# Squares of x on ScalarE and VectorE, most of them in the second column group: a hybrid decoder step on one core

## The chip, the core and the metric

The kernel runs on 1 core of one Trainium2 chip. The metric is the device time of one execution in microseconds; before, it is 1715.74 us, the median of 3 runs (1714.48 to 1716.54). A measurement of this kernel can tell a change of about 0.2% (3.4 us) from none.

## The reference

One step of a decoder layer for 256 prompt rows and 8 sample rows (264 columns in the kernel, which holds everything transposed). Each row is normed, projected to 13 324 columns, mixed by three kinds of head, and projected back:

```python
def rmsnorm(x, g):
    xf = x.astype(F32)
    y = xf * lax.rsqrt(jnp.mean(xf * xf, axis=-1, keepdims=True) + EPS) * g.astype(F32)
...
    aq, ak, av, az, mq, mk, mv, mi, mf, mo, mz, cu, cv, cz = split_projection(
        jnp.einsum('btd,de->bte', hn, w_in))
...
    y = jnp.concatenate([a_out.astype(F32) * jax.nn.silu(az.astype(F32)),
                         m_out * jax.nn.silu(mz.astype(F32)),
                         c_out * jax.nn.silu(cz.astype(F32))], axis=-1).astype(hn.dtype)
    out = jnp.einsum('bte,ed->btd', y, w_out).astype(hn.dtype)
```

The mean of x*x over 4096 features is what this change is about. The factor of the norm is the same for all columns of a row, so the kernel multiplies x by the gain alone, projects it, and applies the factor (`rstd`) to the result.

## The kernel before, in words

The weights come in 34 column groups of 512 columns: 26 of the first projection (`wi`) and 8 of the second (`wo`). A group is worked off in 16 chunks (`NCH`) of two blocks of 128 input features (`KK`), so a chunk is one load of 128 x 1024 weights. `steps` lists all pairs (g, c) of group and chunk, and n counts them through.

Each product is made of three passes with numbers split in two. ScalarE rounds the weights (`wh<-wf`), VectorE takes the rest (`wl<-wf,wh`), and for each of 4 column blocks and 2 feature blocks TensorE multiplies wh by xh, wh by xl and wl by xh: 24 matmuls a chunk, which add up in four PSUM tiles (`mp`) over the 16 chunks of a group. `split_w(n + 2)` stands two chunks ahead of the matmuls; the tiles wf, wh and wl have three buffers each. `load_w(n + 4)` waits on SP's queue until VectorE has made the wl of chunk n + 1, because that frees the buffer.

The first group has more to do, since x comes in with it. Chunk by chunk SP loads two blocks of x into `yb` (`load_x`), ScalarE makes `xh<-yb,sms` (two instructions), and VectorE makes `xl<-yb,sms,xh` (two instructions). `split_x` also squares the two blocks on GpSimd (`sq2<-yb`, in the page `sq`) and adds them up on GpSimd (`acc<-acc,sq`). When the first group is through, `first_norm` sums `acc` over the partitions on TensorE and makes `rstd`. The first group's results went out of PSUM unscaled (`evac` with g == 0: `yb<-mp` on ScalarE), so `first_norm` scales and gates these four tiles; every later group multiplies by rstd as it leaves PSUM (`et<-mp,rstd` on VectorE) and a `gated` task finishes it.

Tiles of yb are used twice: results of group 0 go into tiles 12 to 15, which held the x of chunks 6 and 7, and those of group 1 into tiles 16 to 19, the x of chunks 8 and 9.

The gates of the matrix memory need 12 more columns of the projection. `gate_loads` clears `wgs` on GpSimd and loads `wgf`, `gate_prep` multiplies by the gain on VectorE, and `gate_mm` issues 32 small matmuls (`gps<-yb,wgs`) in the first group. The rest of the kernel's constants (`sms[:, 32:]`: identity, masks, gains) are one load.

Within an engine instructions run in the order written; side tasks (`spawn`) are resumed between the column blocks of the main loop by a tally of issued work. Lines in the profile are mostly L201, the helper through which every operation is issued, so tile names tell the work apart.

Of the kernel before, what the change touches and what calls it, by code (L numbers as in the profile page):

```python
# [12 lines left out]
AF = mybir.ActivationFunctionType  # L13
ALU = mybir.AluOpType
# [6 lines left out]
KT = D // P  # L21
# [6 lines left out]
EPS = 1e-6  # L28
# [38 lines left out]
KK = 2  # L67
# [3 lines left out]
NCH = KT // KK  # L71
# [17 lines left out]
def body(tc, xt, wi, wg, wo, sm, kc, vc, c0, wst, w00, bs, cgain, cbias,  # L89
# [3 lines left out]
    with ExitStack() as ctx:  # L93
# [53 lines left out]
        def tt(eng, out, a, b, op):  # L147
            eng.tensor_tensor(out, a, b, op)
# [9 lines left out]
            return n  # L158

        class Eng:  # L160
            """An engine whose issued work is tallied, so that dependent work is issued when due."""

            def __init__(self, eng, key, fixed, per):
                self.e, self.k, self.f, self.p = eng, key, fixed, per
# [44 lines left out]
        DQ = nc.sync  # L209
# [4 lines left out]
        def load_w(n):  # L214
            if n >= len(steps):
                return
            g, c = steps[n]
            src = wi[g] if g < NG else wo[g - NG]
            t = wp.tile([P, KK, 512], F32, name="wf", bufs=3)
            DQ.dma_start(t, src[:, KK * c:KK * c + KK, :])  # L220
            wf_t[n] = t
# [18 lines left out]
        def split_x(s):  # L240
            if s >= NCH:
                return
            for k in range(KK * s, KK * s + KK):
                if s == 0:
                    V.tensor_scalar(xh[:, k], yb[:, k], sc("ng", k), None, ALU.mult)
                else:
                    A.activation(xh[:, k], yb[:, k], AF.Copy, scale=sc("ng", k))
                V.scalar_tensor_tensor(xl[:, k], yb[:, k], sc("ng", k), xh[:, k].bitcast(F32),
                                       ALU.mult, ALU.subtract)
            sl = yb[:, KK * s:KK * s + KK, :]  # L250
            if s == 0:
                tt(G, acc, sl, sl, ALU.mult)
            else:
                q = ph.tile([P, KK, T], F32, name="sq2", tag="vT")
                tt(G, q, sl, sl, ALU.mult)
                tt(G, acc, acc, q, ALU.add)

        def rsqrt(out, x, scale, v, t):
            """out = (x * scale + EPS) ** -0.5, with one Newton step; v and t are scratch."""
            n = out.shape[0]  # L260
            V.tensor_scalar(v, x, -0.5 * scale, -0.5 * EPS, ALU.mult, ALU.add)
            A.activation(t, x, AF.Sqrt, scale=scale, bias=epsc[:n, 0:1])
            newton(out, v, t)
# [69 lines left out]

        st = {}

# [1 line left out]
        def gate_loads():  # L337
            wgf = ph.tile([P, KT, 12], F32, name="wgf", tag="big", bufs=2)
            wgs = ph.tile([P, KT, 32], F32, name="wgs", tag="big", bufs=2)
            G.memset(wgs, 0.0)  # L340
            DQ.dma_start(wgf, wg)
            st["wgf"], st["wgs"] = wgf, wgs
# [83 lines left out]
            rel()  # L426
            st.update(gd=gd, encol=encol, gcol=gcol)

# [1 line left out]
        def head_loads(h):  # L430
            cb = ph.tile([P, TS, DV + 1], F32, name="cb", bufs=2)
            while h >= 2 and ("done", h - 2) not in st:
# [146 lines left out]
                    tt(V, dst, dst, src[:, :, j], ALU.mult)  # L579
            rel()  # L580

# [1 line left out]
        def attn_kv(g):  # L583
            kT, vT, vtok = st["kT"], st["vT"], st["vtok"]
            ps = yield from acq()
# [136 lines left out]
                tt(V, ys, ys, pnb[:, 24 * g:24 * g + 24].rearrange("p (b j) -> p j b", j=3), ALU.mult)  # L722
            rel()

# [1 line left out]
        def gmlp_prep():  # L726
            wm = ph.tile([P, CG, P], F32, name="wm")
            Z = ph.tile([P, CG, P], F32, name="Z")
# [76 lines left out]
                yield  # L805
                DQ.dma_start(dst, TM[:n, b])

# [1 line left out]
        def gated(kind, i, t):  # L809
            yield 1.5 if kind != "cv" else None  # L810
            s = t
# [29 lines left out]
        def first_norm():  # L841
            yield
            ps = yield from acq()
            yield from wait("es", 2)
            norm_factor(ps, [acc[:, 0], acc[:, 1]])
            rel()
            give("es")
            give("es")
            yield
            for i in range(4):  # L850
                y = yb[:, S_A + i]
                yield from wait("es")
                s = hp.tile([P, T], F32, name="es", bufs=2)
                tt(V, y, y, rstd, ALU.mult)
                yield
                A.activation(s, y, AF.Sigmoid)
                yield
                tt(V, y, y, s, ALU.mult)
                give("es")

        def evac(g, kind, i, ps):
            if g == 0:
                A.activation(yb[:, S_A + i], ps, AF.Copy)
            elif kind in ("mo", "mz", "az", "cz", "cu", "cv"):
                while not free["et"]:
                    tick(True)
                free["et"] -= 1
                t = hp.tile([P, T], F32, name="et", bufs=4)
                tt(V, t, ps, rstd, ALU.mult)
                spawn(gated(kind, i, t), urgent)  # L870
            elif kind == "mq":
                q = ph.tile([P, T], F32, name="q")
                tt(V, q, ps, rstd, ALU.mult)
                st["mq", i] = q
            elif kind == "mk":
                k = ph.tile([P, T], F32, name="k")
                V.scalar_tensor_tensor(k, ps, ISQ, rstd, ALU.mult, ALU.mult)
                st["mk", i] = k
            elif kind == "mv":
                h, f = i  # L880
                if f == 0:
                    st["mv", h] = ph.tile([P, 2, T], F32, name="vt")
                tt(V, st["mv", h][:, f], ps, rstd, ALU.mult)
            elif kind in ("ak", "av"):
                if "kT" not in st:
                    st["kT"] = ph.tile([P, AKV, T], F32, name="kT")
                    st["vT"] = ph.tile([P, AKV, T], F32, name="vT")
                    st["vtok"] = ph.tile([P, AKV, 2, P], F32, name="vtok")
                    st["qs"] = ph.tile([P, AH, TS], F32, name="qs")
                tt(V, st["kT" if kind == "ak" else "vT"][:, i], ps, rstd, ALU.mult)  # L890
            elif kind == "aq":
                q = ph.tile([P, T], F32, name=f"aq{i % 4}")
                V.scalar_tensor_tensor(q, ps, ISQ, rstd, ALU.mult, ALU.mult)
                V.tensor_copy(st["qs"][:, i], q[:, TP:])
                st["aq", i] = q
# [54 lines left out]

        last = []

# [1 line left out]
        def drain():  # L954
            while gens or urgent:
                tick(True)
# [12 lines left out]
        load_w(1)  # L969
        load_x(2)  # L970
        load_w(2)
        DQ.dma_start(sms[:, 32:], sm[:, 32:])
        gate_loads()
        warm = px.tile([P, 512], F32, name="mx")
        for i in range(NWARM):
            PE.matmul(warm[:, :P], ones, ones, start=True, stop=True)
# [7 lines left out]
        for n, (g, c) in enumerate(steps):  # L984
            if c == 0:
                before_group(g)
                main_ps = [pm.tile([P, 512], F32, name="mp") for _ in range(4)]
            if g == 0:
                load_x(c + 4)
            load_w(n + 4)  # L990
            if g == 0:
                split_x(c + 2)
            split_w(n + 2)
            if g == NG:
                for i in (KK * c, KK * c + 1):
                    if i < S_C:
                        nc.sync.dma_start(yb[:, i, :], xt[:, i, :])
            if g == NG - 1 and c >= 1 and KK * (c - 1) < S_C:
                for i in range(KK * (c - 1), KK * c):
                    split_y(i)  # L1000
            if g == NG and KK * c + KK > S_C:
                while ("c", KK * c + KK - 1 - S_C) not in st:
                    tick(True)
            wh, wl = wh_t.pop(n), wl_t.pop(n)
            for j in range(4):
                tick()
                out = main_ps[j][:, :T]
                for kk in range(KK):
                    k = KK * c + kk
                    s = slice(P * j, P * j + P)  # L1010
                    PE.matmul(out, wh[:, kk, s], xh[:, k], start=(k == 0), stop=False)
                    PE.matmul(out, wh[:, kk, s], xl[:, k], start=False, stop=False)
                    PE.matmul(out, wl[:, kk, s], xh[:, k], start=False, stop=(k == KT - 1))
                if c == NCH - 1:
                    if g < NG:
                        kind, i, _ = GROUPS[g][j]
                        evac(g, kind, i, out)
                    else:
                        evac_out(4 * (g - NG) + j, out)
            if g == 0 and c == 4:  # L1020
                gate_prep()
            if g == 0 and c >= 7:
                for m in ([(c - 7) // 2] if c < NCH - 1 else range((c - 7) // 2, KT // 4)):
                    if c % 2:
                        gate_mm(m)
            if c == NCH - 1 and g < NG:
                if g == 0:
                    spawn(chain(first_norm(), gate_sum()), urgent)
                after_group(g)
        drain()  # L1030
# [133 lines left out]
```

## Time and profile before

| | |
|---|---|
| runs, median (lowest to highest) | 1715.74 us (1714.48 to 1716.54) |
| profiled execution, span from first to last instruction | 1715.0 us (the profile gives no other time of that execution) |
| TensorE busy | 1682.7 us, 98% |
| VectorE / ScalarE / GpSimd busy | 928.2 / 733.2 / 125.2 us |
| HBM traffic | 191 GB/s over the span |
| first matmul of group 0, of group 1 | 4.96 us, 73.92 us |

TensorE's busy time takes in matmuls at half clock, so a share of 98% does not say that it ran at its peak. The median of the three runs lies 0.7 us above the span, which is inside the spread of the runs.

### The profile page before, as it was taken

How to read it: one execution, taken by the hardware profiler on the slowest of the kernel's cores; microseconds unless marked ns; L12 is line 12 of the kernel's file. 1: busy time of each engine (PE TensorE's matmuls, PEld its weight loads, DVE VectorE, ACT ScalarE, POOL GpSimd, SP SyncE). 2: the span in 40 equal slices, each digit the busy share in tenths (PEclk: the TensorE clock that was granted, in tenths of full speed). 3: DMA queues.
4: the chain of work that ended last, by engine and by line, in shares of the span. 5: the costliest groups of instructions: out<-in, count | busy, mean ns of one | idle time of the engine just before them, and what ended most of it. 6: DMA issues, size and time to landing. Idle time of an engine off the chain costs nothing.

```text
span 1715.0 us, 32547 instructions
## 1 busy us (share of the span) xinstructions
PE 1682.7 (98%) x13754; PEld 1664.7 (97%) x13754; DVE 928.2 (54%) x1262; ACT 733.2 (43%) x954; POOL 125.2 (7%) x113
## 2 busy tenths in 40 slices
PE   7999999999999999999999999999999999999995
PEld 7899999999999999999999999999999999999995
DVE  8755444555554455555655566444566554444445
ACT  4444433444444334344444444334454443444442
POOL 7300000000000000000101000000100030000002
PEclk9999999999999999999999999999999999999998
DMA  6566668555556666667677767666666666565663
GB/s 225 176 181 175 183 184 264 180 165 155 161 160 176 182 182 176 208 191 237 214 232 220 240 213 221 177 181 184 201 177 216 198 196 190 180 184 177 181 183 145
DMA packets 102178, 328.92 MB, mean 192 GB/s; under 512 B 11090, under 2 KB 24328, under 8 KB 102032
## 3 DMA queue, kind: packets, MB, share of 16 engines
q1 hardware_dynamic: 101072, 326.04, 62.7%
q8 instruction: 107, 1.75, 0.4%
q10 hardware_dynamic: 960, 0.81, 0.1%
q14 instruction: 39, 0.32, 0.1%
HBM read 314.20 MB, written 12.60 MB: 191 GB/s over the span
## 4 chain that ended last, share of the span: by engine, by line
PE 94%; DVE 3%; DMA 1%; issue 1%; ACT 0%; SPq 0%; DVEq 0%; ACTq 0%
PE mp L201 90%; PE mx L201 3%; DVE wl L201 1%; DVE xl L201 1%; DVE yb L201 1%; DMA wf<-wi 1%; DMA wf<-wo 1%; PE sn L201 0%; ACT wh L201 0%; PE gps L201 0%; DVE rstd L201 0%; DVE TM L201 0%; DVE mvs L201 0%; ACT L201 0%; DVE es L201 0%
## 5 line engine op out<-in xcount | busy, mean ns | idle before, releaser
L201 PE MATMUL mp<-xh,wl 128*128 128x264 f32 x4352 | 1240.6, 285 | 12.6 <-DVE wl L201 12.6
L201 PE MATMUL mp<-xh,wh 128*128 128x264 f32 x4352 | 1251.5, 288 | 0.6 <-ACT wh L201 0.6
L201 PE MATMUL mp<-xl,wh 128*128 128x264 f32 x4352 | 1238.2, 285 | 0.0
L201 DVE TENSOR_TENSOR wl<-wf,wh 128x1024 fp32r<-128x1024 f32 (+1 forms) x545 | 695.0, 1278 | 750.8 <-ACT wh L201 746.0
L201 ACT ACTIVATE wh<-wf 128x1024 fp32r<-128x1024 f32 (+1 forms) x545 | 575.0, 1058 | 839.1 <-PE mp L201 734.2
L201 PEld LDWEIGHTS mp<-xh,wl 128*128 128x128 f32 x4352 | 820.6, 189 | 15.2 <-DVE wl L201 15.0
L201 PEld LDWEIGHTS mp<-xh,wh 128*128 128x128 f32 x4352 | 820.7, 189 | 7.2 <-issue 5.0
L201 PEld LDWEIGHTS mp<-xl,wh 128*128 128x128 f32 x4352 | 820.8, 189 | 0.4
L201 POOL TENSOR_TENSOR acc<-acc,es 128x264 f32<-128x264 f32 x29 | 21.9, 754 | 417.1 <-ACT es L201 415.1
L201 POOL TENSOR_SCALAR_AFFINE_SELECT tmp<-bc 128x128 f32<-128x128 f32 x12 | 4.7, 412 | 496.6 <-DMA bc<-gd 496.6
L201 DVE SCALAR_TENSOR_TENSOR xl<-yb,sms,xh 128x264 fp32r<-128x264 f32 x32 | 35.1, 1135 | 1.2 <-ACT xh L201 1.1
L201 ACT ACT_TABLE_LOAD x25 | 32.1, 1283 | 3.4 <-DVE ar L201 2.2
L201 POOL MEMSET pad<- 128x1024 f32 x2 | 1.9, 950 | 406.4 <-PE mx L201 406.4
L201 POOL TENSOR_TENSOR acc<-acc,sq 128x528 f32<-128x528 f32 x15 | 24.0, 1603 | 1.2
L201 ACT ACTIVATE es<-et 128x264 f32<-128x264 f32 x36 | 14.0, 420 | 21.4 <-DVE yb L201 18.1
L201 POOL TENSOR_TENSOR cb<-cb,bc 128x2056 f32<-128x2056 f32 x6 | 21.7, 3616 | 0.0
L201 POOL TENSOR_TENSOR sq<-yb 128x528 f32<-128x528 f32 x15 | 20.6, 1375 | 9.8 <-DMA yb<-xt 9.1
L201 ACT ACTIVATE es<-yb 128x264 f32<-128x264 f32 x33 | 13.6, 412 | 16.3 <-DVE yb L201 16.3
L201 DVE TENSOR_TENSOR et<-mp,rstd 128x264 f32<-128x264 f32 x56 | 20.3, 423 | 0.0
L201 DVE SCALAR_TENSOR_TENSOR cb<-vb,wsk,cb 128x257 f32<-128x257 f32 x48 | 20.1, 480 | 0.0
L201 ACT ACTIVATE bias<-bias,ar 128x128 f32<-128x128 f32 (+1 forms) x24 | 10.7, 448 | 21.4 <-DVE ar L201 21.2
L201 ACT ACTIVATE xh<-yb 128x264 fp32r<-128x264 f32 x32 | 12.1, 412 | 17.7 <-DVE yb L201 17.7
(178 smaller groups left out, 471.6 us busy)
## 6 DMA issues: line engine op xcount, KB each, us to landing
wf<-wi SPq DMA_DIRECT2D x415, 512.0 KB, 3.6
wf<-wo SPq DMA_DIRECT2D x128, 512.0 KB, 3.6
cb<-c SPq DMA_DIRECT2D x12, 514.0 KB
o_cs<-cb SPq DMA_DIRECT2D x12, 514.0 KB, 6.4
vb<-vsd SPq DMA_DIRECT2D x12, 512.0 KB, 5.2
yb<-xt SPq DMA_DIRECT2D x34, 132.0 KB, 3.7
yb<-xt SPq DMA_DIRECT2D x15, 264.0 KB, 5.3
o_y<-yb SPq DMA_DIRECT2D x7, 528.0 KB, 3.1
```

Source lines behind the costliest of these rows:

```text
L201: return fn(*a, **k)
```

## The change

Four things change. The squares are made on ScalarE and added on VectorE by a function of its own, `square_x`; it is called for two pieces at the end of group 0 and for fourteen in the chunks of group 1, the pieces whose tiles are overwritten first. `first_norm` is started after group 1, so the first two groups leave PSUM unscaled (`yb<-mp`) and it finishes eight tiles, not four. The loads of `wgf` and of `sms[:, 32:]` move from the start to chunks 6 and 12 of group 0. And `gate_prep` and `gate_mm` stand later in group 0.

```diff
@@ split_x, and a new function
-            sl = yb[:, KK * s:KK * s + KK, :]
-            if s == 0:
-                tt(G, acc, sl, sl, ALU.mult)
+
+        SQ = [6, 7, 8, 9] + [s for s in range(NCH) if s not in (6, 7, 8, 9)]
+
+        def square_x(n):
+
+            if n >= NCH:
+                return
+            sl = yb[:, KK * SQ[n]:KK * SQ[n] + KK, :]
+            if n == 0:
+                A.activation(acc, sl, AF.Square)
             else:
                 q = ph.tile([P, KK, T], F32, name="sq2", tag="vT")
-                tt(G, q, sl, sl, ALU.mult)
-                tt(G, acc, acc, q, ALU.add)
+                A.activation(q, sl, AF.Square)
+                tt(V, acc, acc, q, ALU.add)
...
@@ first_norm
-            for i in range(4):
+            for i in range(8):
...
@@ evac
-            if g == 0:
+            if g <= 1:
                 A.activation(yb[:, S_A + i], ps, AF.Copy)
...
@@ main sequence
         load_w(2)
-        DQ.dma_start(sms[:, 32:], sm[:, 32:])
-        gate_loads()
...
             load_w(n + 4)
+            if (g, c) == (0, 6):
+                gate_loads()
+            if (g, c) == (0, 12):
+                DQ.dma_start(sms[:, 32:], sm[:, 32:])
             if g == 0:
                 split_x(c + 2)
...
-            if g == 0 and c == 4:
+            if n == NCH - 6:
                 gate_prep()
-            if g == 0 and c >= 7:
-                for m in ([(c - 7) // 2] if c < NCH - 1 else range((c - 7) // 2, KT // 4)):
-                    if c % 2:
-                        gate_mm(m)
+            if g == 0 and c >= NCH - 4:
+                for m in range(2 * (c - NCH + 4), 2 * (c - NCH + 4) + 2):
+                    gate_mm(m)
+            if NCH - 3 <= n <= NCH - 2:
+                square_x(n - NCH + 3)
+            elif n >= NCH:
+                square_x(n - NCH + 2)
             if c == NCH - 1 and g < NG:
-                if g == 0:
+                if g == 1:
                     spawn(chain(first_norm(), gate_sum()), urgent)
```

On GpSimd the program begins as follows (lines with - are those of before, lines without a sign stand in both; acc and sq are the sums and the squares).

```order
 L201 MEMSET epsc 128x1 x2
 L201 MEMSET ones 128x128
 L201 MEMSET wgs 128x1024
-L201 ISA
-L201 TENSOR_TENSOR acc<-yb 128x528
-L201 TENSOR_TENSOR sq_138<-yb 128x528
-L201 TENSOR_TENSOR acc<-acc,sq_138 128x528
-L201 TENSOR_TENSOR sq_156<-yb 128x528
-L201 TENSOR_TENSOR acc<-acc,sq_156 128x528
```

The pairs go on to the sixteenth piece; all 31 instructions are gone from GpSimd, and after the three memsets its next work is the memsets of the gates' tiles.

On ScalarE the end of group 0 and the first chunks of group 1 read as follows (wh are the rounded weights, `yb<-mp` the four results of group 0).

```order
-L201 ACTIVATE wh<-wf 128x1024 x3
+L201 ACTIVATE wh<-wf 128x1024
+L201 ACTIVATE acc<-yb 128x528
+L201 ACTIVATE wh<-wf 128x1024
+L201 ACTIVATE sq_690<-yb 128x528
+L201 ACTIVATE wh<-wf 128x1024
 L201 ACTIVATE yb<-mp 128x264 x4
 L201 ACTIVATE wh<-wf 128x1024
+L201 ACTIVATE sq_769<-yb 128x528
+L201 ACTIVATE wh<-wf 128x1024
+L201 ACTIVATE sq_802<-yb 128x528
```

One square now follows each rounding of weights, from the last chunks of group 0 to chunk 13 of group 1; on VectorE one sum `acc<-acc,sq` of 128x528 follows each `wl<-wf,wh` in the same way.

On SP's queue, before, the first loads after those of chunk 0 are these (x goes to yb, weights to wf).

```order
5 L238 DMA yb<-xt 128x528
6 L220 DMA wf<-wi 128x1024
7 L238 DMA yb<-xt 128x528
8 L220 DMA wf<-wi 128x1024
9 L972 DMA sms<-sm 128x762
10 L341 DMA wgf<-wg 128x384
11 L238 DMA yb<-xt 128x528
12 L220 DMA wf<-wi 128x1024
```

In the changed kernel numbers 9 and 10 are the x and the weights of chunk 3; `wgf` is number 25, behind the weights of chunk 10, and `sms` number 36, behind those of chunk 16.

## Rows read from the trace of the kernel before

**Rows 1.** The page's busy times: busy us, share of the span, instructions of each engine.

```profile
PE 1682.7 (98%) x13754; PEld 1664.7 (97%) x13754; DVE 928.2 (54%) x1262; ACT 733.2 (43%) x954; POOL 125.2 (7%) x113
```

**Rows 2.** Stretches of the trace (start:end, length, busy us and instructions of PE, PEld, DVE, ACT and POOL, granted clock of TensorE, DMA share, GB/s): group 0, groups 4 and 5 (47 us each), then single stretches inside group 0.

```profile
4.96:73.92 68.96, 58.12 (x451) 52.56 (x450) 63.11 (x52) 34.01 (x54) 46.73 (x35) 0.98 0.69 219
221.00:268.00 47.00, 47.00 (x387) 47.00 (x387) 20.97 (x20) 17.23 (x19) 0.00 (x0) 1.00 0.66 194
268.00:315.00 47.00, 47.00 (x387) 46.92 (x385) 21.55 (x24) 18.19 (x20) 0.00 (x0) 1.00 0.82 265
9.00:14.00 5.00, 3.83 (x26) 3.62 (x25) 5.00 (x4) 3.26 (x5) 4.71 (x3) 1.00 1.04 399
28.00:29.00 1.00, 1.00 (x6) 1.00 (x6) 1.00 (x2) 0.05 (x1) 0.92 (x2) 0.50 0.76 78
```

**Rows 3.** What TensorE's matmuls waited for from 0 to 76 us: us in total, times, longest.

```profile
PE mp L201 <- DVE wl L201: 10.8, 9, 1.8
```

**Rows 4.** The same from 76 us to the end.

```profile
PE mp L201 <- DVE wl L201: 1.7, 2, 1.6
```

**Rows 5.** VectorE's instructions in order of time at two places of group 0: start, duration of the merged instructions, operation.

```profile
10.66 2.07 DVE L201 TENSOR_TENSOR wl<-wf,wh 128x1024 fp32r<-128x1024 f32 x1
12.66 2.77 DVE L201 SCALAR_TENSOR_TENSOR xl<-yb,sms,xh 128x264 fp32r<-128x264 f32 x2
...
44.35 1.55 DVE L201 SCALAR_TENSOR_TENSOR xl<-yb,sms,xh 128x264 fp32r<-128x264 f32 x1
45.82 1.21 DVE L201 TENSOR_TENSOR wl<-wf,wh 128x1024 fp32r<-128x1024 f32 x1
46.96 0.88 DVE L201 SCALAR_TENSOR_TENSOR xl<-yb,sms,xh 128x264 fp32r<-128x264 f32 x2
```

**Rows 6.** GpSimd's instructions at the same two places.

```profile
10.52 1.14 POOL L201 TENSOR_TENSOR sq<-yb 128x528 f32<-128x528 f32 x1
11.74 2.19 POOL L201 TENSOR_TENSOR acc<-acc,sq 128x528 f32<-128x528 f32 x1
...
44.22 1.40 POOL L201 TENSOR_TENSOR acc<-acc,sq 128x528 f32<-128x528 f32 x1
48.47 1.43 POOL L201 TENSOR_TENSOR sq<-yb 128x528 f32<-128x528 f32 x1 [2.86 <-DMA yb<-xt]
```

**Rows 7.** TensorE's matmuls in order of time: the last before and the first behind the wait in chunk 1, the first and last of a stretch of fifteen start-to-start steps, a lot of gate matmuls (`x8` records for four instructions), the last lot (`x32` records for sixteen), and the first matmul of group 1.

```profile
11.34 0.28 PE L201 MATMUL mp<-xl,wh 128*128 128x264 f32 x1
12.79 0.39 PE L201 MATMUL mp<-xh,wl 128*128 128x264 f32 x1 [1.17 <-DVE wl L201]
...
27.61 0.39 PE L201 MATMUL mp<-xh,wh 128*128 128x264 f32 x1
...
30.88 0.37 PE L201 MATMUL mp<-xh,wh 128*128 128x264 f32 x1
...
65.39 0.65 PE L201 MATMUL gps<-yb,wgs 128*32 128x264 f32 x8
...
71.99 2.00 PE L201 MATMUL gps<-yb,wgs 128*32 128x264 f32 x32
73.92 0.39 PE L201 MATMUL mp<-xh,wh 128*128 128x264 f32 x1
```

**Rows 8.** ScalarE's roundings of the weights of chunk 1, and of the x and weights of chunk 3.

```profile
9.57 1.06 ACT L201 ACTIVATE wh<-wf 128x1024 fp32r<-128x1024 f32 x1 [0.72 <-DMA wf<-wi]
...
13.67 0.92 ACT L201 ACTIVATE xh<-yb,sms 128x264 fp32r<-128x264 f32 x2 [1.09 <-DMA yb<-xt]
14.99 1.06 ACT L201 ACTIVATE wh<-wf 128x1024 fp32r<-128x1024 f32 x1 [0.40 <-DMA wf<-wi]
```

**Rows 9.** A piece of the chain that ended last: start, length, and a whole group of matmuls without a break.

```profile
219.88 46.86 PE mp L201 x384
```

**Rows 10.** DMA issues on SP's queue in order of time.

```profile
4.55 0.57 SPq L972 DMA_DIRECT2D sms<-sm  x1
...
6.48 0.67 SPq L238 DMA_DIRECT2D yb<-xt  x1
7.37 0.33 SPq L220 DMA_DIRECT2D wf<-wi  x1
...
12.77 0.33 SPq L220 DMA_DIRECT2D wf<-wi  x1
```

**Rows 11.** DMA issues by form: KB each, median us from issue to landing.

```profile
wf<-wi SPq DMA_DIRECT2D x415, 512.0 KB, 3.6
...
yb<-xt SPq DMA_DIRECT2D x15, 264.0 KB, 5.3
...
sms<-sm SPq DMA_DIRECT2D x1, 381.0 KB, 7.9
```

**Rows 12.** Groups of VectorE's instructions by shape from 73.92 to 315 us: busy us, mean ns of one, and idle time ahead of them.

```profile
L201 DVE TENSOR_TENSOR wl<-wf,wh 128x1024 fp32r<-128x1024 f32 x81 | 99.2, 1225 | 117.1 <-ACT wh L201 117.1
...
L201 DVE TENSOR_TENSOR yb<-yb,es 128x264 f32<-128x264 f32 x4 | 1.7, 427 | 0.0
```

**Rows 13.** The same for ScalarE from 0 to 315 us.

```profile
L201 ACT ACTIVATE yb<-mp 128x264 f32<-128x264 f32 x4 | 1.5, 387 | 0.9 <-PE mp L201 0.9
...
L201 ACT ACTIVATE wh<-wf 128x512 fp32r<-128x512 f32 x2 | 1.3, 630 | 3.1 <-DMA wf<-wi 3.1
```

**Rows 14.** The last instruction that makes rstd, on VectorE.

```profile
79.94 0.43 DVE L201 SCALAR_TENSOR_TENSOR rstd<-es,rstd 128x264 f32<-128x264 f32 x1
```

## The prediction

> **What bounds the kernel now.** First the page's busy times: TensorE is busy 98% of the span, every other engine 54% or less [rows 1]. So the time is that of the matmuls, and only stretches in which TensorE stands still or runs slowly can give anything back. Next the waits: TensorE waited 10.8 us for `wl` in nine pieces before 76 us [rows 3], and 1.7 us for it in all the rest [rows 4]. The place is group 0. Then the stretches: a whole group later is 384 matmuls in 46.86 us, 0.122 us each [rows 9], while group 0 takes 68.96 us from its first matmul to the first of group 1; there VectorE is busy 63.11 us of 68.96 and GpSimd 46.73 us, and in groups 4 and 5 VectorE is busy 21 to 22 us of 47 with GpSimd at nothing [rows 2].
>
> Why VectorE is full there is seen by laying its row beside GpSimd's. While GpSimd squares and adds, `wl` takes 2.07 us and a pair of `xl` 2.77 us. From 45.62 to 48.47 us GpSimd waits for data, and the same two take 1.21 and 0.88 us [rows 5, 6]. One `xl` starts at 44.35 us, 0.13 us after a GpSimd sum of 1.40 us began, and ends at 45.90, 0.28 us after it [rows 5, 6]: VectorE seems to stand until GpSimd is through. So a chunk in group 0 costs VectorE up to 2.07 + 2.77 = 4.8 us beside GpSimd, and 2.1 us alone, against 24 x 0.122 = 2.93 us on TensorE. VectorE is the bound in the first case and not in the second.
>
> The Trainium skill says the same of the cause ("SBUF — State Buffer", Who interferes with whom): VectorE with two SBUF inputs and a GpSimd instruction that reads SBUF contend for one port pair, an exclusive lock, and the loser blocks until the other is through. By that rule the memsets left on GpSimd, which read nothing, would cost VectorE nothing; no term below hangs on it.
>
> **The change, part by part.** *The squares leave GpSimd.* TensorE's first matmul that needs `wl` of chunk 1 starts at 12.79 us [rows 7]. The `wl` before it starts at 10.66 us, behind a rounding from 9.57 to 10.63 us that waited for its weights [rows 5, 8]; this start stays. The `wl` then takes 1.225 us as in the later groups [rows 12], so the matmul starts at 10.66 + 1.225 + 0.06 = 11.94 us (0.06 is the distance from the end of `wl`, 12.73, to the matmul now). From there 358 matmuls of group 0 are left (15 chunks of 24 less the two of chunk 1 that need no `wl`): 358 x 0.122 = 43.7 us. The 32 gate matmuls stay; before they are four lots of four at 0.65 us and one of sixteen at 2.00 us, 4.6 us [rows 7]. After, they are four lots of eight; on the line between 0.65 and 2.00 a lot of eight takes 1.10 us, together 4.4 us. Behind each of five breaks the next matmul comes about 0.1 us late (0.39 us long instead of 0.28), 0.5 us. Group 1 then starts at 11.94 + 43.7 + 4.4 + 0.5 = 60.5 us instead of 73.92: **13.4 us less**. This holds only if no chunk waits any more.
>
> The half clock goes with the waits. From 27.61 to 30.88 us matmuls follow each other at 0.22 us, at a granted clock of 0.50, that is 1.2 GHz [rows 2, 7], right behind the fourth long wait; 15 steps cost 1.5 us too much, and they are inside the 13.4. As a check from the waits: 10.8 idle, less about 0.9 that stays in chunk 0 (its `wl` waits for the second half of its weights) and 0.3 that stays in chunk 1, plus 1.5 for the clock, plus some 0.25 us of refilling behind each of seven waits that go (in chunk 1, 12.79 - 11.34 - 1.17 less one step of 0.12, and 0.11 on the matmul after), gives 12.9 us.
>
> *Will a chunk wait for something else?* In steady state `wh` of chunk n + 2 starts when chunk n - 1 is through (its buffer), `wl` ends 1.06 + 1.22 = 2.3 us later, and chunk n + 2 starts 5.9 us after that start: 3.6 us to spare. The load of chunk n + 5 goes out with the end of this `wl`, and its rounding is due at 3 x 2.93 = 8.8 us, so it may take 6.5 us; loads of weights took 3.6 us, those of x 5.3 us [rows 11]. ScalarE has 1.06 + 0.92 us of work in 2.93 [rows 8]. So transfers have the least to spare, 1.2 us.
>
> *The constants load later.* 573 KB (381 of `sms`, and 128 x 384 numbers of `wgf`) leave the head of the queue; x and weights of chunk 3 go out at 4.55 and 7.37 us instead of 6.48 and 7.37 [rows 10]. At the 399 GB/s of that stretch [rows 2] they land up to 1.5 us earlier. The rounding of chunk 3 waited 0.40 us for its weights and ended at 16.05 us [rows 8], and chunk 3 will not start before 11.94 + 46 x 0.122 = 17.6 us, so this alone gives nothing: 0, with 0.5 us as the upper bound if the weights of chunk 1 had shared the transfer with the constants (the wait that is left in chunk 1). Later `wgf` is issued behind the weights of chunk 10; `gate_prep` stands on VectorE behind `wl` of chunk 12, five chunks or 14.6 us after, more than the 7.9 us that the largest constant took at the start [rows 11]. Hidden; without that cover VectorE would stand for the difference, once. `sms` stands ahead of the weights of chunk 17 only and can hold them up by its own 381 KB, 1 us, against 1.2 us to spare.
>
> *Squares and sums in group 1.* A square of 528 columns on ScalarE lies between 264 at 0.39 and 512 at 0.63 us [rows 13]; by size 0.65 us. A sum of 528 on VectorE lies between 264 at 0.43 and 1024 at 1.225 us [rows 12]; 0.70 us. A chunk then has 1.06 + 0.65 = 1.7 us on ScalarE and 1.225 + 0.70 = 1.9 us on VectorE, both inside 2.93 us: cost nothing. Queued behind a waiting sum is the next `wl`, with 3.6 us to spare.
>
> *The norm a group later.* rstd was ready at 80.37 us, 6.5 us into group 1 [rows 14]; it will be ready as far into group 2 and is needed when group 2 leaves PSUM, 40 us later. Four results leave through ScalarE at 0.39 us each instead of VectorE, and four more are scaled and gated afterwards: side work, cost nothing.
>
> Sum: 1715.0 - 13.4 = 1701.6 us of span. The median of the runs lies 0.7 us above the span, so 1702.3 us.
>
> **The rivals.** *Transfers become the bound* (10%). Group 0 needs 776 KB each 2.93 us, 271 GB/s, more than any whole group moves now: 265 GB/s in group 5, 219 in group 0 [rows 2]. At 265 a chunk takes 3.00 us, 1.0 us more over 14 chunks: 1703.3. At 219 it takes 3.63 us, 9.8 us more: 1712.1. Against it speak 399 GB/s over 5 us of the same transfers [rows 2], and that group 5 loses nothing at 265. I take 240 GB/s as this case, 3.31 us, 5.3 us more: 1707.6.
> The Trainium skill has a rule that speaks for this rival ("DMA: Bandwidth & Descriptors", Measured): small transfers do not reach the rate of large ones, 0.95 us for 64 KB and 6.15 us for 1 MB. On a line through these a chunk's 264 and 512 KB would take 2.0 + 3.4 = 5.4 us, an estimate from that page, and nothing would be gained. The trace does not bear it out: sixteen such chunks would be 86 us, and group 0 takes 69.
>
> *The change doesn't do what it says* (4%): VectorE's instructions are long in group 0 for another reason than GpSimd, say the incoming x. Then `wl` and `xl` stay long and the time stays at 1715.5. For it: all the long `wl` stand in group 0. Against it: the short ones at 45.82 and 46.96 us stand there too, just where GpSimd pauses.
>
> *Slower* (4%): in group 1 the square and the sum form one chain with the splitting, since each sum holds up VectorE's queue until ScalarE has squared. If a chunk had to go through rounding, `wl`, square and sum one after the other, with the sum as long as the longest on GpSimd, 2.19 us [rows 6], it would be 1.06 + 1.22 + 0.65 + 2.19 = 5.1 us, 2.2 over; 14 chunks cost 30.8 us: 1733. It decides against the gain from 2.93 + 13.4/14 = 3.9 us a chunk. Against it: the next rounding waits for TensorE and not for the sum, and GpSimd, which made the sum long, is idle.
>
> **How the numbers follow.** The forecast's own case has 78%, 1702.3 us, with 1700.7 to 1704.5: down by the 0.5 us of the constants and 1 us if the clock rises earlier, up by some small waits. Transfers 10%, no effect 4%, slower 4%; 4% are left for waits in the next groups, half of them still faster. Some transfers would end below 1706.5, so 1700.5 to 1706.5 holds 8 in 10. A measurement of this kernel can tell 0.2%, 3.4 us, from no change: faster 0.91, same 0.05, slower 0.04.
>
> **What would show it.** Right: GpSimd without work in group 0, every `wl` there at 1.21 to 1.23 us and `xl` near 0.45, group 1 starting near 60.5 us, no half clock after the start, matmuls waiting for `wl` by less than 2.5 us in group 0. In group 1 squares near 0.65 and sums near 0.70 us, and no wait of TensorE. Wrong: roundings of weights in group 0 that wait for their loads while TensorE waits for `wl` (transfers); `wl` above 2 us without GpSimd; a group 1 longer than 48 us.

## The result and the profile after

The changed kernel takes 1702.89 us, the median of four runs (1702.04 to 1703.58), against 1716.14 us (1714.48 to 1716.71) for the kernel before in the same session: a ratio of 0.9926, with a 95% interval from 0.9914 to 0.9938. It is 13.2 us faster. The forecast was 1702.3 us, inside 1700.5 to 1706.5. The profiled execution's span is 1701.9 us, against 1715.0 for the kernel before.

The page's busy times, to be laid beside [rows 1]:

```profile
PE 1678.2 (99%) x13754; PEld 1662.2 (98%) x13754; DVE 909.4 (53%) x1277; ACT 739.2 (43%) x971; POOL 80.7 (5%) x82
```

VectorE has 15 instructions more than before and is busy 19 us less. It was given more work and is busy for less time, so the time that it lost was not work.

Stretches of the changed kernel (columns as in [rows 2]): most of group 0 (it runs from 4.74 to 60.62 us), the part of it behind 11.40 us, and group 1 with most of the squares.

```profile
4.96:60.00 55.04, 53.08 (x441) 49.92 (x443) 35.84 (x53) 33.50 (x55) 1.38 (x4) 0.97 0.81 272
11.40:60.60 49.20, 49.20 (x430) 46.20 (x429) 32.26 (x47) 30.68 (x49) 1.38 (x4) 1.00 0.78 261
60.00:107.50 47.50, 47.50 (x400) 47.01 (x389) 28.28 (x30) 25.48 (x34) 0.00 (x0) 1.00 0.55 172
```

From 11.40 us to the end of group 0 TensorE is busy 49.20 us of 49.20 at the full granted clock, and so it is in group 1. VectorE, busy 63.11 us of 68.96 in group 0 before, is now busy 35.84 us of 55.04, and GpSimd, 46.73 us before, 1.38 us.

VectorE's instructions by shape from 10.5 to 60 us (columns as in [rows 12]), and then in order of time where [rows 5] has its first pair:

```profile
L201 DVE TENSOR_TENSOR wl<-wf,wh 128x1024 fp32r<-128x1024 f32 x17 | 20.8, 1226 | 15.0 <-ACT wh L201 15.0
L201 DVE SCALAR_TENSOR_TENSOR xl<-yb,sms,xh 128x264 fp32r<-128x264 f32 x28 | 12.5, 488 | 0.0
```

```profile
10.58 1.23 DVE L201 TENSOR_TENSOR wl<-wf,wh 128x1024 fp32r<-128x1024 f32 x1 [0.87 <-ACT wh L201]
11.72 0.89 DVE L201 SCALAR_TENSOR_TENSOR xl<-yb,sms,xh 128x264 fp32r<-128x264 f32 x2
```

All seventeen `wl` are short, not only those in a pause of GpSimd; VectorE now waits 15.0 us for ScalarE there, so it has room.

TensorE's matmuls in order of time: the last two of the three waits of chunk 0, the first matmul of chunk 1 that needs `wl`, one lot of gate matmuls, and the first matmul of group 1.

```profile
7.36 0.39 PE L201 MATMUL mp<-xh,wh 128*128 128x264 f32 x1 [0.77 <-ACT wh L201]
8.09 0.59 PE L201 MATMUL mp<-xh,wl 128*128 128x264 f32 x1 [0.21 <-DVE wl L201]
...
12.18 0.28 PE L201 MATMUL mp<-xh,wl 128*128 128x264 f32 x1
...
47.17 1.10 PE L201 MATMUL gps<-yb,wgs 128*32 128x264 f32 x16
...
60.62 0.39 PE L201 MATMUL mp<-xh,wh 128*128 128x264 f32 x1
```

Group 1 starts at 60.62 us instead of 73.92 [rows 7]: 13.3 us, and that is the whole gain (the span is 13.1 us shorter). What TensorE's matmuls still waited for, from 0 to 62 us (answering to [rows 3]):

```profile
PE mp L201 <- DVE wl L201: 1.2, 2, 1.0
...
PE mp L201 <- ACT wh L201: 0.8, 1, 0.8
```

and from 62 us to the end (answering to [rows 4]):

```profile
PE mp L201 <- DVE wl L201: 1.4, 2, 1.2
PE mp L201 <- DVE et L201: 0.5, 1, 0.5
PE mp L201 <- ACT wh L201: 0.3, 1, 0.3
```

The line with `et` has no counterpart before. VectorE and TensorE at that place, the end of group 2:

```profile
153.56 1.23 DVE L201 TENSOR_TENSOR wl<-wf,wh 128x1024 fp32r<-128x1024 f32 x1 [1.67 <-ACT wh L201]
154.70 0.43 DVE L201 TENSOR_TENSOR yb<-yb,es 128x264 f32<-128x264 f32 x1
155.05 0.43 DVE L201 TENSOR_TENSOR yb<-yb,rstd 128x264 f32<-128x264 f32 x1
155.39 1.45 DVE L201 TENSOR_TENSOR et<-mp,rstd 128x264 f32<-128x264 f32 x4
```

```profile
155.96 0.36 PE L201 MATMUL mp<-xh,wh 128*128 128x264 f32 x1 [0.54 <-DVE et L201]
```

The first result of group 2 leaves PSUM only behind the gating of one (`yb<-yb,es`) and the scaling of another (`yb<-yb,rstd`) of the eight tiles that `first_norm` finishes, and the next group's first matmul waits 0.54 us for that PSUM tile.

### The profile page after: what moved, and what is told of

It reads as the page before. It is cut to its first block, busy times and chain, and to the rows that moved or that the text cites. A ratio compares the mean times of both kernels' runs of the same rounds, so it can differ in the third digit from the quotient of the medians.

```text
span 1701.9 us, 32534 instructions
## 1 busy us (share of the span) xinstructions
PE 1678.2 (99%) x13754; PEld 1662.2 (98%) x13754; DVE 909.4 (53%) x1277; ACT 739.2 (43%) x971; POOL 80.7 (5%) x82
## 3 DMA queue, kind: packets, MB, share of 16 engines
q8 instruction: 107, 1.75, 0.4%
## 4 chain that ended last, share of the span: by engine, by line
PE 97%; DVE 1%; DMA 1%; ACT 0%; issue 0%; SPq 0%; DVEq 0%; ACTq 0%
PE mp L201 93%; PE mx L201 3%; DVE yb L201 1%; DMA wf<-wo 1%; PE sn L201 0%; DVE wl L201 0%; DMA wf<-wi 0%; PE gps L201 0%; ACT wh L201 0%; DVE rstd L201 0%; DVE TM L201 0%; DVE mvs L201 0%; ACT L201 0%; DVE es L201 0%; SPq L973 0%
## 5 line engine op out<-in xcount | busy, mean ns | idle before, releaser
L201 DVE TENSOR_TENSOR wl<-wf,wh 128x1024 fp32r<-128x1024 f32 (+1 forms) x545 | 686.4, 1263 | 756.8 <-ACT wh L201 750.4
L201 ACT ACTIVATE yb<-yb,sms 128x264 f32<-128x264 f32 x32 | 16.5, 517 | 1.0
L201 DVE TENSOR_TENSOR yb<-yb,rstd 128x264 f32<-128x264 f32 x32 | 16.1, 558 | 0.0
L201 DVE SCALAR_TENSOR_TENSOR xl<-yb,sms,xh 128x264 fp32r<-128x264 f32 x32 | 14.4, 489 | 0.8 <-ACT xh L201 0.8
```

The costliest lines, as they stand in the source:

```text
L201: return fn(*a, **k)
```

## The experiments

The theory: in group 0 VectorE stands while GpSimd reads for its squares and sums; all of the gain comes from taking these off GpSimd, and neither their place in group 1, nor the loads of the constants, nor the gates' place bears on the time. The first rival puts the gain into the other parts of the change (constants and gates out of the way, the place in group 1); a second one says that any work on GpSimd, or on a core just loading x, lengthens VectorE's.

### 1. Constants and gates alone

```diff
@@ main sequence of the kernel before
-        DQ.dma_start(sms[:, 32:], sm[:, 32:])
-        gate_loads()
...
+            if (g, c) == (0, 6):
+                gate_loads()
+            if (g, c) == (0, 12):
+                DQ.dma_start(sms[:, 32:], sm[:, 32:])
...
-            if g == 0 and c == 4:
+            if n == NCH - 6:
                 gate_prep()
-            if g == 0 and c >= 7:
-                for m in ([(c - 7) // 2] if c < NCH - 1 else range((c - 7) // 2, KT // 4)):
-                    if c % 2:
-                        gate_mm(m)
+            if g == 0 and c >= NCH - 4:
+                for m in range(2 * (c - NCH + 4), 2 * (c - NCH + 4) + 2):
+                    gate_mm(m)
```

> The kernel before with the constants alone moved: wgf and sms load in chunks 6 and 12, gate_prep and gate_mm stand late in group 0; the squares stay on GpSimd. Theory (GpSimd holds up VectorE in group 0): wl still takes 2.07 to 2.35 us beside GpSimd, group 1 starts between 73.2 and 74.0 us, the time is 1715 to 1716.5 us. Rival (the loads at the start hold the kernel up): at least 2 us of the 13.2 come here, group 1 starts before 72 us, the time is 1714 us or less.

Measured: 1717.28 us against 1716.18, ratio 1.0005 (0.9995 to 1.0015). What the matmuls waited for from 0 to 202 us, and the first matmul of group 1:

```profile
PE mp L201 <- DVE wl L201: 11.0, 7, 1.8
```

```profile
76.00 0.39 PE L201 MATMUL mp<-xh,wh 128*128 128x264 f32 x1
```

The waits for `wl` stay at 11 us. Group 1 starts 2.1 us later than in [rows 7], and the time is 0.8 us over the 1716.5 us of the theory: both are later than it had expected. After the first 12 us TensorE's matmuls follow each other at 0.22 us in three stretches of 15 or 16 steps, from 17.66, 28.15 and 58.76 us, where the kernel before has one such stretch [rows 7]. One of the three (columns as in [rows 2]; the granted clock is 0.50):

```profile
58.80:62.20 3.40, 3.40 (x18) 3.40 (x17) 3.40 (x4) 0.26 (x1) 3.07 (x6) 0.50 0.53 154
```

Two more, at about 1.5 us each, are more than the 2.1 us. They come behind three of the four waits of 1.75 to 1.77 us here, and behind one of the three of 1.73 to 1.77 us in the kernel before; why not behind each stays open. These parts of the change give nothing by themselves.

### 2. Constants and gates' loads back at the start

```diff
@@ main sequence of the changed kernel
+        DQ.dma_start(sms[:, 32:], sm[:, 32:])
+        gate_loads()
...
-            if (g, c) == (0, 6):
-                gate_loads()
-            if (g, c) == (0, 12):
-                DQ.dma_start(sms[:, 32:], sm[:, 32:])
```

> The changed kernel with the loads of wgf and sms back at the start. Theory: nothing but a later chunk 3 or so, group 1 starts between 60.6 and 61.6 us, the time is 1702.5 to 1704 us. Rival (transfers of the start are worth something once VectorE is free): group 1 starts after 62.5 us, the time is over 1704.7 us.

Measured: 1703.64 us, ratio 0.9927 (0.9912 to 0.9941); group 1 starts at 60.44 us. With the constants early nothing is lost: the later load is worth nothing that can be measured, in either direction.

### 3. The squares on ScalarE and VectorE, but left in group 0

```diff
@@ split_x of the kernel before
-                tt(G, acc, sl, sl, ALU.mult)
+                A.activation(acc, sl, AF.Square)
...
-                tt(G, q, sl, sl, ALU.mult)
-                tt(G, acc, acc, q, ALU.add)
+                A.activation(q, sl, AF.Square)
+                tt(V, acc, acc, q, ALU.add)
```

> The kernel before with the engines alone changed: squares on ScalarE and sums on VectorE, where they were, in group 0; constants and norm as before. Theory (the engine counts, not the place): per chunk VectorE has 1.23 + 0.89 + 0.70 = 2.8 us and ScalarE 1.06 + 0.91 + 0.63 = 2.6 us, both inside 2.93, so most of the gain comes here too: some 1 to 2 us of it is lost at the start, where each chunk waits for splitting, and the time is 1703 to 1706 us. Rival (the place counts): with 2.8 of 2.93 us VectorE falls behind in each chunk, TensorE waits for wl as before, and the time is over 1709 us.

Measured: 1703.73 us, ratio 0.9926 (0.9911 to 0.9940). VectorE in group 0, two chunks:

```profile
26.93 0.70 DVE L201 TENSOR_TENSOR acc<-acc,sq 128x528 f32<-128x528 f32 x1
27.55 1.21 DVE L201 TENSOR_TENSOR wl<-wf,wh 128x1024 fp32r<-128x1024 f32 x1
28.69 0.89 DVE L201 SCALAR_TENSOR_TENSOR xl<-yb,sms,xh 128x264 fp32r<-128x264 f32 x2
29.49 0.70 DVE L201 TENSOR_TENSOR acc<-acc,sq 128x528 f32<-128x528 f32 x1
```

VectorE does more work a chunk than before (0.70 + 1.21 + 0.89 = 2.8 us by durations, which overlap a little: from sum to sum it is 29.49 - 26.93 = 2.56 us), has no pause here, and still keeps below the 2.93 us of TensorE; from 40 us on it waits for `wh` again. Group 1 starts at 61.50 us, 0.9 later than in the changed kernel, but no wait for `et` follows, and the time is the same. So the engine is what counts; the place in group 1 gives nothing that can be measured.

### 4. The changed order with the squares and sums on GpSimd

```diff
@@ square_x of the changed kernel
-                A.activation(acc, sl, AF.Square)
+                tt(G, acc, sl, sl, ALU.mult)
...
-                A.activation(q, sl, AF.Square)
-                tt(V, acc, acc, q, ALU.add)
+                tt(G, q, sl, sl, ALU.mult)
+                tt(G, acc, acc, q, ALU.add)
```

> The changed kernel with squares and sums on GpSimd again, but where they now stand, mostly in group 1. Theory (a collision costs only where VectorE has no time to spare): wl in group 1 takes 1.2 to 2.6 us, has 3.6 us to spare there, TensorE does not wait, rstd comes some 10 to 15 us later, the time is 1702 to 1704 us. Rival (squares on GpSimd cost wherever they stand): each of 14 chunks of group 1 loses about 0.9 us as in group 0, the time is 1712 us or more.

Measured: 1716.77 us, ratio 1.0004 (0.9994 to 1.0013). The theory's number fell. GpSimd in order of time, with the last sum:

```profile
24.01 2.19 POOL L201 TENSOR_TENSOR acc<-acc,sq 128x528 f32<-128x528 f32 x1
...
43.31 2.19 POOL L201 TENSOR_TENSOR acc<-acc,sq 128x528 f32<-128x528 f32 x1
...
68.89 2.18 POOL L201 TENSOR_TENSOR acc<-acc,sq 128x528 f32<-128x528 f32 x1
```

Group 1 starts only at 73.87 us here, so the work that the program has in group 1 was done in group 0. Nothing stood ahead of it in GpSimd's queue, so it ran as soon as its x was there, from 20.04 us on. Beside it VectorE is as slow as before:

```profile
42.23 2.08 DVE L201 TENSOR_TENSOR wl<-wf,wh 128x1024 fp32r<-128x1024 f32 x1
44.24 2.76 DVE L201 SCALAR_TENSOR_TENSOR xl<-yb,sms,xh 128x264 fp32r<-128x264 f32 x2
```

The run therefore doesn't test the place. It shows that a later place in the program did not move the work on an engine whose queue holds nothing ahead of it; ScalarE's queue, full of roundings, does hold it in the changed kernel. The next runs hold or replace the work.

### 5. GpSimd as busy as before, but reading nothing

```diff
@@ split_x of the kernel before
-                tt(G, acc, sl, sl, ALU.mult)
+                G.memset(acc, 4.0)
...
-                tt(G, q, sl, sl, ALU.mult)
-                tt(G, acc, acc, q, ALU.add)
+                for _ in range(5):
+                    G.memset(q, 0.0)
```

> The kernel before with every square and sum on GpSimd replaced by memsets of the same tiles, five of 528 columns for a pair (about 0.5 us each), so that GpSimd is busy beside VectorE in group 0 about as long but reads nothing; the sum of squares, and with it the factor of the norm, is left out. The memsets wait for no data, so they stand from 2 us on without a break. Theory (VectorE is held up by what GpSimd reads): wl stays at 1.2 to 1.3 us beside the memsets, group 1 starts near 61 us, the time is 1702 to 1704 us. Rival (any work on GpSimd holds VectorE up): wl and xl are 2 us and more beside them and the time is over 1709 us.

Measured: 1703.38 us, ratio 0.9923 (0.9908 to 0.9938). GpSimd and VectorE by shape from 0 to 62 us:

```profile
L201 POOL MEMSET sq<- 128x528 f32 x75 | 40.6, 542 | 4.3
L201 DVE TENSOR_TENSOR wl<-wf,wh 128x1024 fp32r<-128x1024 f32 x18 | 22.1, 1225 | 17.7 <-ACT wh L201 17.6
L201 DVE SCALAR_TENSOR_TENSOR xl<-yb,sms,xh 128x264 fp32r<-128x264 f32 x32 | 14.4, 489 | 1.8 <-ACT xh L201 1.7
```

GpSimd is busy 40.6 us in these memsets, which stand from 2.4 to 47.2 us, and `wl` takes 1225 ns as if it were idle. x comes in as before, too. Both forms of the second rival fall: neither a busy GpSimd nor the incoming x lengthens VectorE's instructions. What does is something that a square or a sum on GpSimd does and a memset doesn't, and its reading of SBUF is the nearest; no run here separates the reading from the arithmetic. The rule of the Trainium skill ("SBUF — State Buffer", Who interferes with whom) is that a GpSimd instruction which only writes doesn't contend with VectorE's second input; the trace agrees, with 1225 ns.

### 6. The squares on GpSimd, held back to group 1

A small tile that ScalarE writes in its queue's order, and that GpSimd reads before each square, keeps GpSimd at the place in the program.

```diff
@@ square_x of the changed kernel, ahead of the squares and sums on G as in 4
+            tok = hp.tile([P, 2], F32, name="tok", bufs=4)
+            A.activation(tok, epsc, AF.Copy)
+            tt(G, tok, tok, tok, ALU.add)
```

> The run with squares on GpSimd in the second group again, but held there: before each square ScalarE writes a tile of two columns behind the rounding of that chunk, and GpSimd reads it first, so that GpSimd cannot start before. Theory (a collision costs only where VectorE has no time to spare): wl in group 1 goes up to 2.0 to 2.6 us, has 3.6 us to spare, TensorE does not wait, group 1 starts near 61 us, the time is 1702 to 1705 us. Rival (squares on GpSimd cost wherever they stand): group 1 takes 55 us or more instead of 48, the time is 1709 us or more.

Measured: 1710.0 us, ratio 0.9960 (0.9947 to 0.9972). VectorE and GpSimd at one place of group 1:

```profile
83.23 2.38 DVE L201 TENSOR_TENSOR wl<-wf,wh 128x1024 fp32r<-128x1024 f32 x1 [1.18 <-ACT wh L201]
...
89.13 2.08 DVE L201 TENSOR_TENSOR wl<-wf,wh 128x1024 fp32r<-128x1024 f32 x1 [1.36 <-ACT wh L201]
```

```profile
83.22 1.32 POOL L201 TENSOR_TENSOR acc<-acc,sq 128x528 f32<-128x528 f32 x1
84.49 1.18 POOL L201 TENSOR_TENSOR tok<-tok 128x2 f32<-128x2 f32 x1
...
88.92 0.19 POOL L201 TENSOR_TENSOR tok<-tok 128x2 f32<-128x2 f32 x1
```

Here the long `wl` stand in group 1, where no x comes in, and matmuls waited for none of them from 60 to 110 us: beside 24 matmuls a `wl` of 2.4 us is hidden. So far the theory holds.

The trace of the kernel before had the same far behind group 0. Between 765 and 1023 us GpSimd runs six `cb<-cb,bc` of 3.62 us, the `wl` beside them take 3.4 to 4.0 us, no x is loaded, and no matmul waits from 700 to 1100 us. The first of the six:

```profile
765.12 3.62 POOL L201 TENSOR_TENSOR cb<-cb,bc 128x2056 f32<-128x2056 f32 x1
```

```profile
766.23 3.59 DVE L201 TENSOR_TENSOR wl<-wf,wh 128x1024 fp32r<-128x1024 f32 x1 [1.71 <-ACT wh L201]
```

In (6) the theory also expected 1702 to 1705 us and was wrong there, for the chain of the norm is late. TensorE at the start of group 2:

```profile
110.52 0.28 PE L201 MATMUL mp<-xh,wl 128*128 128x264 f32 x1
114.59 1.16 PE L201 MATMUL mx<-acc,ones 128*128 128x264 f32 x4 [3.79 <-POOL acc L201]
...
116.16 0.42 PE L201 MATMUL mp<-xl,wh 128*128 128x264 f32 x1
...
119.02 0.42 PE L201 MATMUL mp<-xh,wl 128*128 128x264 f32 x1
```

GpSimd needs about 3.5 us for `tok`, square and sum, and falls behind. The norm's matmul waits in TensorE's queue for the last sum, with the rest of group 2 behind it, 3.8 us; then fourteen steps, from 116.16 to 119.24 us, at 0.22 instead of 0.122 us (granted clock 0.50 from 116 to 118 us) cost 1.4 more. With group 1 starting 0.9 us later (61.50) this is 6.1 of the 6.5 us by which the span (1708.4 us) is longer than the changed kernel's.

### 7. A half dose: only the sums on GpSimd, in group 0

```diff
@@ split_x of the kernel before
-                tt(G, acc, sl, sl, ALU.mult)
+                A.activation(acc, sl, AF.Square)
...
-                tt(G, q, sl, sl, ALU.mult)
+                A.activation(q, sl, AF.Square)
                 tt(G, acc, acc, q, ALU.add)
```

> The kernel before with the squares on ScalarE in group 0 and only the sums left on GpSimd: one GpSimd instruction of 1.4 us a chunk instead of two. Theory (VectorE stands until the GpSimd instruction is through): one instruction can hold VectorE up by at most its own 1.4 us, so a chunk takes VectorE 2.1 to 3.5 us and TensorE waits by up to 0.6 us in some chunks; the time is 1704 to 1711 us. Rival (both run at a reduced rate side by side): 2.1 + 0.7 = 2.8 us, inside 2.93, and 1702 to 1704 us.

Measured: 1706.57 us, ratio 0.9942 (0.9927 to 0.9956); group 1 starts at 63.27 us. VectorE and GpSimd:

```profile
28.71 2.03 DVE L201 SCALAR_TENSOR_TENSOR xl<-yb,sms,xh 128x264 fp32r<-128x264 f32 x2
30.66 1.21 DVE L201 TENSOR_TENSOR wl<-wf,wh 128x1024 fp32r<-128x1024 f32 x1
...
33.68 1.21 DVE L201 TENSOR_TENSOR wl<-wf,wh 128x1024 fp32r<-128x1024 f32 x1
```

```profile
29.12 1.32 POOL L201 TENSOR_TENSOR acc<-acc,sq 128x528 f32<-128x528 f32 x1 [0.76 <-ACT sq L201]
...
33.82 2.25 POOL L201 TENSOR_TENSOR acc<-acc,sq 128x528 f32<-128x528 f32 x1 [0.76 <-ACT sq L201]
```

One GpSimd instruction a chunk holds up one `xl` of the pair (2.03 us instead of 0.89). The other collision goes the other way: at 33.82 us the `wl` was first, and the sum took 2.25 us. VectorE's chunk, from `wl` to `wl`, is 33.68 - 30.66 = 3.02 us, a little over TensorE's 2.93, and the time lies between the kernels before and after, as the theory had it. The waits are not as it had them: instead of up to 0.6 us in some chunks there is one of 0.78 us in chunk 1 and one of 1.51 us at 31.93 us, after `gate_prep` had taken 1.67 us on VectorE beside a sum (0.55 us in the changed kernel).

## Why the prediction was right, and where it was off

- **GpSimd holds VectorE up, and this bounds group 0: shown.** Take the squares and sums off GpSimd by a change of engine in place (3), or put memsets there (5), and the time is 1703.4 to 1703.7 us; leave them, and move the rest (1), and it is 1717.3; leave only the sums (7), and it lies between. That it is their reading is argued from (5).
- **The start in chunk 1: 0.24 us too early.** The `wl` ended at 10.58 + 1.23 = 11.81 us, as forecast (11.88), but the matmul ran at 12.18, not 11.94, without a wait. The step took TensorE to be ready by then, as in [rows 7]; instead chunk 0 ended later, since the rounding of the second half of its weights started at 6.68 us (5.98 before) and a wait of 0.77 us for `wh` came up that was not foreseen:

```profile
6.68 0.63 ACT L201 ACTIVATE wh<-wf 128x512 fp32r<-128x512 f32 x1 [2.08 <-DMA wf<-wi]
```

  In the check from the waits, the 0.9 us that stay in chunk 0 became 2.0 (0.99, 0.77 and 0.21), and the 0.3 us of chunk 1 became none. The rounding starts anywhere from 6.1 to 6.5 us in (1) to (6), with the constants in either place, so it isn't laid to the change; why it varies stays open.
- **358 matmuls and the gate lots: right.** From 12.18 to 60.62 us are 48.4 us; 43.7 + 4.4 + 0.5 = 48.6 was forecast. These 0.2 us less and the start 0.24 us late nearly cancel: that group 1 starts within 0.1 us of the forecast is in part luck. The gate lots of eight took the 1.10 us that was interpolated.
- **The half clock: right.** From 11.40 us on the granted clock of group 0 is 1.00.
- **The transfers: hidden, as forecast, but their slack of 1.2 us was not there.** Three roundings between 16 and 23 us waited about 1 us each for weights, such as the first of these rows of ScalarE; later ones wait for TensorE, as the second does. The loads of these three went out at 11.83, 13.79 and 15.81 us and took 4.5 to 6.4 us, where the forecast had 3.6; x took 7.1 us on the page, where it had 5.3.

```profile
16.30 1.06 ACT L201 ACTIVATE wh<-wf 128x1024 fp32r<-128x1024 f32 x1 [0.97 <-DMA wf<-wi]
...
32.46 1.06 ACT L201 ACTIVATE wh<-wf 128x1024 fp32r<-128x1024 f32 x1 [1.05 <-PE mp L201]
```

  No matmul waited behind them: the 3.6 us that a rounding and its `wl` have to spare hid what the loads were late. Group 0 moved 272 GB/s where 271 were needed, above the 265 and 219 of the rival of the transfers, which falls.
- **The constants: 0, right** (1 and 2). `gate_prep` ran at 40.59 us, behind a load issued at 26.88.
- **Squares and sums in group 1: right**, and no matmul waits there. By shape, from 62 to 107.5 us, 0.63 and 0.70 us:

```profile
L201 DVE TENSOR_TENSOR acc<-acc,sq 128x528 f32<-128x528 f32 x14 | 9.8, 702 | 0.0
...
L201 ACT ACTIVATE sq<-yb 128x528 f32<-128x528 f32 x13 | 8.2, 629 | 0.0
```

  The rival on the other side, which put these into one chain, thus has nothing to show for it.
- **The rival of no effect: falls with (5), but its reason was read wrongly.** The prediction says that all the long `wl` stand in group 0. Six of 3.4 to 4.0 us stand between 766 and 1024 us in the trace of the kernel before, without x and beside GpSimd (rows under 6). They speak against this rival, and for the theory, before any run.
- **The norm a group later "costs nothing": 0.54 us too little.** rstd was ready in time, at 114.22 + 0.43 us. What the step left out is that the eight tiles finished afterwards stand on VectorE in front of what empties PSUM. The wait is there, at 0.5 us, in every run with the norm behind group 1, (2), (4) and (6), and in none with the norm behind group 0, (1), (3), (5) and (7).
- **The sum:** 1701.6 us of span were forecast, 1701.9 measured; the 0.1 us of a later group 1 and the 0.5 us of `et` are in it. The median lies 1.0 us above this span, not 0.7. This term sets the median of several runs against the span of one: each of the four runs lies 1.7 to 2.0 us above its own span, and the profiled one was the slowest of them (1703.58 us). So the term is no property of the kernel, and its size is within the spread of the runs.

## What to carry to other kernels

When an engine is full in a stretch, compare the length of one instruction there with the same shape elsewhere before counting its work: here up to 4.8 us a chunk were 2.1 us of work and 2.7 us of standing beside GpSimd, and handing VectorE more work made the kernel faster. Work moved in the program stays there only if something holds it; on GpSimd, idle in (4), it started as soon as its data were in. And a side chain may be late as long as it has no instruction of its own in the queue of the engine that bounds (3.8 us in 6), nor stands ahead of what empties that engine's PSUM (0.54 us in the changed kernel).

## What the hardware showed beyond that

- The length of a collision goes by what is left of the other engine's instruction, not by one's own size: a GpSimd instruction of two columns took 0.19 us with VectorE idle, and 1.18 us when it came up during a `wl`, ending at 85.67 us, 0.06 after that (6).
- Whoever comes second stands, on either side: `wl` 1.21 and the sum 2.25 us at one place, `xl` late and the sum 1.32 us at another (7).
- The granted clock that the trace lists for the first 11 us doesn't go with the pace: in the kernel before it is 1.00 from 7 to 10.4 us, while matmuls follow each other mostly at 0.22 us; in the changed kernel it is 0.50 from 8.5 to 11.1 us, at the same pace.
